# Strassen's scheme for the second product of a feed-forward stage

## The chip, the cores and the metric

One core of a Trainium2 chip. The metric is the device time of one execution in microseconds. A core has TensorE (matmuls, with a weight load before each), VectorE, ScalarE, GpSimd, and SyncE (SP), which here issues nearly all transfers. Memory on the chip is SBUF (128 partitions) and eight PSUM banks of 128 x 512 float32, into which TensorE accumulates.

## The reference

Five transformer layers in eight stages on 512 tokens of width 1024: `dil`, `diff`, `ev`, `x0`, `ff0`, `sw`, `x1`, `ff1`. The change touches the two feed-forward stages:

```
def squared_relu_mlp(u, w1, w2):
    return jnp.square(jax.nn.relu(u @ w1)) @ w2
...
        u = squared_relu_mlp(rms_norm(h, g_ff_pre[l]), w_ff1[l], w_ff2[l])
        h = h + rms_norm(u, g_ff_post[l])
```

Here `w1` is 1024 x 4096 and `w2` 4096 x 1024, so `y = relu(u w1)^2` is 512 x 4096. With float32 needed, each product is made of three: an operand is split into `hi` (rounded to the matmul's type) and `lo` (the rest), and hi hi, hi lo and lo hi are added (`mm3`).

## The kernel before

The weights come in one stream (`stream_order`, packed by the host as `ws[n]`, 128 x 2048): `cols` tiles are eight row blocks of 128 by 256 columns, `rows` tiles four row blocks by 512 columns. `weights(key)` (L262) hands out tile n, makes hi and lo of tile n+1 (`_split`, L249: ScalarE copies 1024 columns, VectorE subtracts, twice) and has tile n+2 loaded (`_dma`, L239: two transfers of 512 KB on SP through three `raw` buffers). `whi` and `wlo` are two buffers each of a whole tile.

A unit (`unit`, L307) is 128 features of the first product for all 512 tokens: 24 matmuls of 512 columns with the weights stationary. The first four units of a stage are begun (`begin`, L331) for tokens 0 to 255 at the end of the stage before it, while tokens 256 to 511 still go through the norm; `unit` then does the other half.

`ff` (L1211) works in four quarters q of 1024 features. In each, eight units are squared (ScalarE L1222, VectorE L1223) and split (`split_y`, L358); then the second product of this quarter is made for columns 0 to 511 and 512 to 1023 (c), in halves of the depth (kh), for four token tiles t, with four k each: 128 tokens of `y` stationary, 512 columns of weights moving. Each of its sums is added to `acc` in SBUF (VectorE L1247). In the last quarter, columns 512 to 1023 go through `second_half` (L462): a token tile at a time is finished, and `boundary` (L414) makes its norm and residual; the transposes of the next stage's input (`norm_T`, L382) are steps that are run between matmuls (L481, L485) and in `begin` (L350 and L347). `begin_out` (L434) loads the two gains.

Tile's framework makes all semaphores and the order on each engine; buffers of a tag are handed out as they fall free. GpSimd does part of the norms (L390, L376 to L379) and the rotations (L513) of other stages.

## Time and profile before

| what | value |
|---|---|
| median of 3 runs | 2400.42 us (2399.62 to 2403.36) |
| the profiled execution | 2402.01 us |
| its span, first to last instruction | 2400.2 us |
| granted TensorE clock, mean | 0.998 |
| busy: TensorE, VectorE, ScalarE, GpSimd | 2349.0, 1278.6, 930.4, 269.9 us |
| `ff0` lies at | about 1345 to 1702 us |
| `ff1` lies at | about 2053 to 2400 us |

A line of a group of instructions gives source line, engine, operation, out<-in, shapes and count, then busy time, the mean duration in ns, and the idle time before them with what ended it. A view of one line or tile gives durations as min/median/max in ns. A line of the timeline gives start and duration in us; a bracket at its end is the idle time before it and who ended it. Matmuls are pipelined: a listed duration of 0.39 us is not the time a matmul takes from the next; starts tell that.

### The profile page before, as it was taken

The page shows a single profiled execution, that of the slowest core. Times are in us where ns is not written, and L with a number is a line of the kernel's source. Part 1 is how long each engine was busy: PE and PEld are TensorE (multiplying, and loading weights), DVE is VectorE, ACT ScalarE, POOL GpSimd, SP SyncE. Part 2 cuts the span into 40 slices and gives each one's busy share as a digit, 9 for nine tenths or more (in the row PEclk, how much of TensorE's full clock was granted, in tenths as well). Part 3 has the DMA queues.
Part 4 walks back from the last instruction along what each step waited for, and adds up shares of the span by engine and source line. Part 5 has one row for each costly group of instructions (what it writes and reads, how often), then busy time and mean ns, then how long its engine had stood idle before and what let it go on. Part 6 is the DMA issues. An engine that isn't in the chain of part 4 may idle for free.

```text
span 2400.2 us, 33303 instructions
## 1 busy us (share of the span) xinstructions
PE 2349.0 (98%) x13008; PEld 1947.0 (81%) x13008; DVE 1278.6 (53%) x2370; ACT 930.4 (39%) x1843; POOL 269.9 (11%) x315
## 2 busy tenths in 40 slices
PE   7999999999999999999999999999999999999998
PEld 7879788787888878877988888888866988888887
DVE  5364655546665546664644633435786645533434
ACT  3333333333444444453533422323465534432322
POOL 3010111101211112000200100000211201000000
PEclk9999999999999999999999999999999999999999
DMA  5433333334232322223331332322322422332322
GB/s 167 129 102 119 98 116 91 108 93 129 99 100 86 98 91 93 76 70 114 123 123 71 106 101 92 104 90 88 99 84 97 141 89 80 106 105 89 103 90 79
DMA packets 94172, 242.39 MB, mean 101 GB/s; under 512 B 26700, under 2 KB 30828, under 8 KB 94016
## 3 DMA queue, kind: packets, MB, share of 16 engines
q1 hardware_dynamic: 93216, 238.34, 30.4%
q8 instruction: 102, 1.67, 0.3%
q0 software_dynamic: 800, 1.94, 0.3%
q14 instruction: 54, 0.44, 0.1%
HBM read 215.98 MB, written 4.33 MB: 92 GB/s over the span
## 4 chain that ended last, share of the span: by engine, by line
PE 63%; DVE 4%; issue 2%; ACT 2%; POOL 2%; DMA 1%; SPq 0%; POOLq 0%; DVEq 0%; ACTq 0%
PE pj L282 14%; PE pj L284 13%; PE pj L283 13%; PE sc L282 3%; PE sc L283 3%; PE sc L284 3%; PE pv L282 2%; PE pv L284 2%; PE pv L283 2%; PE sc L1325 1%; DVE h L431 1%; PE sc L775 1%; DVE wlo L258 1%; PE pv L797 1%; PE pt L401 1%
## 5 line engine op out<-in xcount | busy, mean ns | idle before, releaser
L258 DVE TENSOR_TENSOR wlo<-raw,whi 128x1024 fp32r<-128x1024 f32 x372 | 473.4, 1294 | 498.0 <-ACT whi L257 498.0
L257 ACT ACTIVATE whi<-raw 128x1024 fp32r<-128x1024 f32 x372 | 382.7, 1055 | 538.7 <-PE pj L284 216.7
L282 PE MATMUL pj<-uh,whi 128*128 128x512 f32 (+1 forms) x1424 | 561.4, 394 | 0.8 <-ACT ho L1101 0.8
L284 PE MATMUL pj<-uh,wlo 128*128 128x512 f32 (+1 forms) x1424 | 551.8, 388 | 1.6 <-DVE wlo L258 1.6
L283 PE MATMUL pj<-ul,whi 128*128 128x512 f32 (+1 forms) x1424 | 550.6, 387 | 0.0
L282 PEld LDWEIGHTS pj<-uh,whi 128*128 128x128 f32 x1424 | 267.6, 188 | 73.7 <-issue 17.1
L284 PEld LDWEIGHTS pj<-uh,wlo 128*128 128x128 f32 x1424 | 267.6, 188 | 60.0 <-issue 3.8
L283 PEld LDWEIGHTS pj<-ul,whi 128*128 128x128 f32 x1424 | 267.9, 188 | 52.1 <-issue 2.4
L513 POOL TENSOR_TENSOR ro<-rt 128x512 f32<-128x512 f32 x74 | 112.8, 1535 | 657.6 <-DVE rt L511 587.9
L282 PE MATMUL pj<-whi,uh 128*128 128x256 f32 x608 | 174.9, 288 | 0.0
L283 PE MATMUL pj<-wlo,uh 128*128 128x256 f32 x608 | 172.5, 284 | 0.0
L284 PE MATMUL pj<-whi,ul 128*128 128x256 f32 x608 | 171.9, 283 | 0.0
L282 PE MATMUL pj<-whi,yh 128*128 128x512 f32 x416 | 164.1, 395 | 1.4 <-ACT yh L355 1.1
L283 PE MATMUL pj<-wlo,yh 128*128 128x512 f32 x416 | 162.6, 391 | 0.9 <-DVE wlo L258 0.9
L284 PE MATMUL pj<-whi,yl 128*128 128x512 f32 x416 | 162.6, 391 | 0.0
L376 POOL TENSOR_SCALAR rs<-ss 128x1 f32<-128x1 f32 x32 | 23.1, 722 | 1089.0 <-ACT bq L422 1088.8
L282 PE MATMUL sc<-whi,yh 128*128 128x512 f32 x320 | 126.8, 396 | 0.1
L283 PE MATMUL sc<-wlo,yh 128*128 128x512 f32 x320 | 125.8, 393 | 0.0
L284 PE MATMUL sc<-whi,yl 128*128 128x512 f32 x320 | 125.2, 393 | 0.0
L282 PEld LDWEIGHTS pj<-whi,uh 128*128 128x128 f32 x608 | 116.4, 191 | 4.6 <-ACT at L231 2.3
L283 PEld LDWEIGHTS pj<-wlo,uh 128*128 128x128 f32 x608 | 116.5, 192 | 0.5 <-issue 0.2
L284 PEld LDWEIGHTS pj<-whi,ul 128*128 128x128 f32 x608 | 116.4, 192 | 0.2 <-issue 0.2
(364 smaller groups left out, 3833.4 us busy)
## 6 DMA issues: line engine op xcount, KB each, us to landing
raw<-in_ws_dram SPq DMA_DIRECT2D x372, 512.0 KB, 4.0
qk<-ro SPq DMA_DIRECT2D x256, 64.0 KB, 2.0
gpre<-in_gains_dram SPq DMA_DIRECT2D x8, 512.0 KB, 5.6
gpost<-in_gains_dram SPq DMA_DIRECT2D x8, 512.0 KB, 5.2
xt<-in_x_dram SPq DMA_DIRECT2D x4, 512.0 KB, 8.1
dv<-v SPq DMA_DIRECT2D x4, 512.0 KB, 4.1
v<-dv SPq DMA_DIRECT2D x16, 128.0 KB, 4.7
h<-in_x_dram SPq DMA_DIRECT2D x4, 512.0 KB, 5.6
```

The lines of the kernel that those rows point to most:

```text
L257: self.nc.scalar.activation(out=hi[:, s], in_=t, func=AF.Copy)
L258: self.nc.vector.tensor_sub(out=lo[:, s], in0=t, in1=hi[:, s].bitcast(F32))
L282: self.nc.tensor.matmul(ps, lhsT=ah, rhs=bh, start=first and k == 0, stop=False)
L283: self.nc.tensor.matmul(ps, lhsT=ah, rhs=bl, start=False, stop=False)
L284: self.nc.tensor.matmul(ps, lhsT=al, rhs=bh, start=False, stop=last and k == n - 1)
L376: nc.gpsimd.tensor_scalar(out=r[:, 0:1], in0=ss[:, 0:1], scalar1=ss[:, 1:2], scalar2=EPS, op0=ALU.add, op1=ALU.add)
L401: nc.tensor.transpose(pt[:, k * P:(k + 1) * P], b[:, (4 * g + k) * P:(4 * g + k + 1) * P], self.ident)
L431: nc.vector.scalar_tensor_tensor(out=h, in0=b, scalar=r, in1=h, op0=ALU.mult, op1=ALU.add)
L513: nc.gpsimd.tensor_tensor(out=o, in0=t[0], in1=t[1], op=op)
L775: nc.tensor.matmul(ps[:, :n], lhsT=q[hs, 0, i * P:n], rhs=q[hs, 1, :n], start=True, stop=True)
L797: nc.tensor.matmul(o[:, i * P:(i + 1) * P], lhsT=at[:, j * P:(j + 1) * P], rhs=v[h // 2][:, j, (h % 2) * P:(h % 2 + 1) * P], start=j == 0, ...
L1325: nc.tensor.matmul(ps[e][:, hp * 256 + lo:(hp + 1) * 256], lhsT=q[hs, hp, i * P:(i + 1) * P], rhs=kd[hs, g, (i - 1) * P + lo:(i + 1) * P], ...
```

## The change

The second product C = y W is cut into halves in tokens (256), in depth (each block of 512 features into two times 256) and in columns (512), and the eight half products become seven (Strassen's scheme in Winograd's form). With A11, A12 for tokens 0 to 255 and A21, A22 for tokens 256 to 511, S1 = A21 + A22, S2 = S1 - A11, S3 = A11 - A21, S4 = A12 - S2; T1 = B12 - B11, T2 = B22 - T1, T3 = B22 - B12, T4 = B21 - T2. The products are A11 B11, A12 B21, S1 T1 (first phase) and S4 B22, S2 T2, S3 T3, A22 T4 (second phase).

- The stage runs in eight blocks q of 512 features. `operands` squares with two ScalarE passes, keeps S2, S3, S4 and A22 of all features in SBUF, makes the four sums on GpSimd and splits A11, A12 and S1. `products(q - 1)` follows the four units of q and accumulates its three products over all depth in six PSUM banks.
- `block` loads the four quarters of a weight block, and GpSimd makes T3, T1, T2 and, once B21 is split, T4. `block_end` stores T2, T3, T4 to DRAM. The second phase reads them back through the weight stream, with B22 from `ws` again; its 32 steps accumulate on top of A11 B11's two banks (S2, S3, A22) or in two of their own (S4).
- The weight stream is handled in halves (`_load`, `_fill`, `_take`): four `whi` and `wlo` buffers of 1024 columns, with a loading depth of 2, or 3 inside `ff`.
- Tokens 0 to 255 get their `boundary` after S2, tokens 256 to 511 after A22, whose steps 3 and 5 hold the transposes of the first two token tiles. The scratch for descriptors of GpSimd's transfers is set to 4096.

```diff
@@ -84,10 +84,11 @@
         elif st in ("ff0", "ff1"):
-            for q in range(4):
-                for j in range(4):
-                    span("ff1_" + st[2], q * 1024 + j * 256)
-                outw("ff2_" + st[2], q * 1024)
+            for q in range(8):
+                for j in range(2):
+                    span("ff1_" + st[2], q * 512 + j * 256)
+                for m in range(2):
+                    out.append(("ff2_" + st[2], "quad", (q * 512 + m * P, m)))
...
         if kind == "cols":
             b = a[:, list(sel)].reshape(8, P, 256)
+        elif kind == "quad":
+
+            b = np.stack([a[sel[0] + 256 * j:sel[0] + 256 * j + P, 512 * c:512 * (c + 1)] for c in range(2) for j in range(2)])
...
+class Halved:
+
+
+    def __init__(self, parts):
+        self.parts = parts
+        self.n = parts[0].shape[1]
+
+    def __getitem__(self, key):
+        p, k, c = key
+        return self.parts[k // self.n][p, k % self.n, c]
+
+
@@ -195,6 +211,19 @@
         self.pos = 0
         self.wt = {}
+
+        self.halves, self.ready, self.loaded, self.done, self.depth = [], [], 0, 0, 2
+        blocks = []
+        for n, (_, kind, sel) in enumerate(self.order):
+            if kind != "quad":
+                self.halves += [(n, 0), (n, 1)]
+            elif sel[1] == 0:
+                blocks.append(n)
+                self.halves += [(b, name) for b in blocks[-2:-1] for name in ("B11", "T1", "B21")]
+                if len(blocks) == 8:
+                    late = [(b, name + "'") for name in ("B22", "T2", "T3", "T4") for b in blocks]
+                    self.halves += late[:5] + [(n, name) for name in ("B11", "T1", "B21")] + late[5:]
+                    blocks = []
...
 
-    def _dma(self, n):
...
-    def _split(self, n):
...
+    def _load(self):
+
+        while self.loaded < len(self.halves) and self.loaded < self.done + self.depth:
+            n, name = h = self.halves[self.loaded]
+            self.loaded += 1
+            if isinstance(name, str) and name[-1] != "'":
+                continue
+            r = self.wt[h] = self.wp.tile([P, 1024], F32, tag="raw", name="raw", bufs=3)
+            if name == "B22'":
+                src = self.a["ws"][n + 1, :, 1024:]
+            elif isinstance(name, str):
+                src = self.wt[n][name]
+            else:
+                src = self.a["ws"][n, :, name * 1024:(name + 1) * 1024]
+            self.nc.sync.dma_start(out=r, in_=src)
+
+    def _fill(self, m):
+
+        while len(self.ready) < m and self.done < len(self.halves):
+            self._load()
+            n, name = h = self.halves[self.done]
+            t = self.wt.pop(h) if h in self.wt else self.wt[n][name]
+            hi = self.wp.tile([P, 1024], F32R, tag="whi", name="whi", bufs=4)
+            lo = self.wp.tile([P, 1024], F32R, tag="wlo", name="wlo", bufs=4)
+            self.parts((hi, lo), t)
+            self.ready.append((hi, lo))
+            self.done += 1
+        self._load()
+
+    def _take(self, m, more=2):
+        self._fill(m + more)
+        got, self.ready = self.ready[:m], self.ready[m:]
+        return got
 
         self.pos += 1
-        self._split(n)
-        self._split(n + 1)
-        self._dma(n + 2)
-        hi, lo = self.wt.pop(n)
+        got = self._take(2)
         c = 256 if self.order[n][1] == "cols" else 512
-        return n, hi.rearrange("p (k c) -> p k c", c=c), lo.rearrange("p (k c) -> p k c", c=c)
-
-    def mm3(self, ps, pairs, first=True, last=True, between=None):
+        return n, *(Halved([g[x].rearrange("p (k c) -> p k c", c=c) for g in got]) for x in range(2))
+
+    def block(self, n, pool):
+
+        q = self.wt[n] = {}
+
+        def new(name):
+            q[name] = pool.tile([P, 1024], F32, tag="quad", name="quad", bufs=5)
+
+        for m, name in enumerate(("B11", "B12", "B21", "B22")):
+            new(name)
+            self.nc.sync.dma_start(out=q[name], in_=self.a["ws"][n + m // 2, :, (m % 2) * 1024:(m % 2 + 1) * 1024])
+        new("T3")
+        q["T1"], q["T2"], q["T4"] = q["B12"], q["B22"], q["B21"]
+        self.less(q["T3"], q["B22"], q["B12"])
+        self.less(q["T1"], q["B12"], q["B11"])
+        self.less(q["T2"], q["B22"], q["T1"])
+
+    def less(self, out, x, y):
+        self.nc.gpsimd.tensor_tensor(out=out, in0=x, in1=y, op=ALU.subtract)
+
+    def block_end(self, n):
+
+        q = self.wt[n]
+        self.less(q["T4"], q["B21"], q["T2"])
+        for name in ("T3", "T2", "T4"):
+            d = q[name + "'"] = self.dr.tile([P, 1024], F32, tag=name, name=name, bufs=8)
+            self.nc.sync.dma_start(out=d, in_=q[name])
+
+    def mm3(self, ps, pairs, first=True, last=True, between=None, **kw):
 
         n = len(pairs)
         for k, ((ah, al), (bh, bl)) in enumerate(pairs):
...
+            self.nc.tensor.matmul(ps, lhsT=ah, rhs=bh, start=first and k == 0, stop=False, **kw)
+            self.nc.tensor.matmul(ps, lhsT=ah, rhs=bl, start=False, stop=False, **kw)
+            self.nc.tensor.matmul(ps, lhsT=al, rhs=bh, start=False, stop=last and k == n - 1, **kw)
...
-    def begin(self, stage, last):
+    def begin(self, stage, last, tags=("sc", "sc", "pj", "pv")):
...
-            ps = self.ps(("sc", "sc", "pj", "pv")[n])
+            ps = self.ps(tags[n])
...
+        d = self.pair()
+        self.parts(d, y)
+        return d
+
+    def pair(self):
+        return [self.yp.tile([P, S], F32R, tag=t, name=t, bufs=8) for t in ("yh", "yl")]
 
...
-    def end_out(self):
+    def end_out(self, **kw):
         if self.next:
             self.u = self.u_next
-            self.begin(self.next, self.steps)
+            self.begin(self.next, self.steps, **kw)
...
 
     def ff(self, l, stage):
-        nc = self.nc
...
+        nc = self.nc
+        h = slice(0, 256), slice(256, S)
+        blocks = [self.order.index((f"ff2_{l}", "quad", (q * 512, 0))) for q in range(8)]
+        outer, inner, first = (ExitStack() for _ in range(3))
+        p = outer.enter_context(self.pool(f"ff{l}"))
+        self.depth = 3
+        left = {n: p.tile([P, 16, 256], F32, name=n) for n in ("S3", "A22")}
+        self.block(blocks[0], p)
+        p2 = inner.enter_context(self.pool(f"fs{l}"))
+        left.update({n: p2.tile([P, 16, 256], F32, name=n) for n in ("S4", "S2")})
+        p1 = first.enter_context(self.pool(f"fr{l}"))
+        banks = {}
+
+        def square(out, ps, tmp):
+            nc.scalar.activation(out=tmp, in_=ps, func=AF.Relu)
+            nc.scalar.activation(out=out, in_=tmp, func=AF.Square)
+
+        def operands(w, n, x2):
+
+            ps = self.unit(w, 0)
+            ya = p1.tile([P, S], F32, tag="ya", name="ya", bufs=2)
+            square(ya, ps, ya)
+            ps = self.unit(w, 1)
+            yb = p1.tile([P, 256], F32, tag="yb", name="yb", bufs=2)
+            square(yb, ps[:, h[0]], yb)
+            square(left["A22"][:, n], ps[:, h[1]], left["A22"][:, n])
+            s1 = p1.tile([P, 256], F32, tag="s1", name="s1", bufs=3)
+            for out, x, z, op in ((s1, ya[:, h[1]], left["A22"][:, n], ALU.add), (left["S2"][:, n], s1, ya[:, h[0]], ALU.subtract),
+                                  (left["S3"][:, n], ya[:, h[0]], ya[:, h[1]], ALU.subtract),
+                                  (left["S4"][:, n], yb, left["S2"][:, n], ALU.subtract)):
+                nc.gpsimd.tensor_tensor(out=out, in0=x, in1=z, op=op)
+            x1 = self.pair()
+            res = {"A11": [z[:, h[0]] for z in x1], "A12": [z[:, h[1]] for z in x1], "S1": [z[:, h[n % 2]] for z in x2]}
+            for name, src in (("A11", ya[:, h[0]]), ("A12", yb), ("S1", s1)):
+                self.parts(res[name], src)
+            return res
+
+        def products(q, ops):
+            for name in ("A11", "S1", "A12"):
+                (hi, lo), = self._take(1)
+                hi, lo = (z.rearrange("p (k c) -> p k c", c=512) for z in (hi, lo))
+                if q == 0:
+                    banks[name] = [self.ps(tag) for tag in {"A11": ("sc", "sc"), "A12": ("pt", "pt"), "S1": ("pv", "pj")}[name]]
+                for t in range(2):
+                    tok = slice(t * P, (t + 1) * P)
+                    self.mm3(banks[name][t], [([z[:, tok] for z in ops[j][name]], (hi[:, j, :], lo[:, j, :])) for j in range(2)],
+                             first=q == 0, skip_group_check=True)
+            self.block_end(blocks[q])
+            if q < 7:
+                self.block(blocks[q + 1], p)
+
+        ops = []
+        for q in range(8):
+            x2 = self.pair()
+            new = [operands(self.weights(f"ff1_{l}"), 2 * q + j, x2) for j in range(2)]
+            self.pos += 2
+            if q:
+                products(q - 1, ops)
+            ops = new
+        banks["S4"] = [self.ps("pj") for _ in range(2)]
+        acc, bo, late = {}, [], []
+        part = lambda t, c: acc[t][:, c * 512:(c + 1) * 512]
+        add = lambda out, ps: nc.vector.tensor_tensor(out=out, in0=out, in1=ps, op=ALU.add)
+
+        def done(name, t):
+            ps = banks[name if name == "S4" else "A11"][t]
+            if name in ("S4", "S2"):
+                add(part(t, 1), ps)
+            if name == "S2":
+                self.boundary(t, (part(t, 0), part(t, 1)), self.h[:, t, :], stage, bo[0])
+            elif name == "S3":
+                add(part(2 + t, 1), ps)
+            elif name == "A22":
+                self.boundary(2 + t, (ps, part(2 + t, 1)), self.h[:, 2 + t, :], stage, bo[0])
+
+        def go(name, i, t, y, w):
+            self.mm3(banks[name if name == "S4" else "A11"][t],
+                     [([z[:, j * 256 + t * P:j * 256 + (t + 1) * P] for z in y], [z[:, j, :] for z in w]) for j in range(2)],
+                     first=name == "S4" and i == 0, skip_group_check=True)
+            if i == 7:
+                done(name, t)
+
+        steps = [(name, i) for name in ("S4", "S2", "S3", "A22") for i in range(8)]
+
+        def split(k):
+            name, i = steps[k]
+            return self.split_y(left[name][:, 2 * i:2 * i + 2, :].rearrange("p k t -> p (k t)"))
+
+        ys = [split(0)]
+        for k, (name, i) in enumerate(steps):
+            if k == 5:
+                products(7, ops)
+                first.close()
+                acc.update({t: p.tile([P, D], F32, tag="quad", name="acc", bufs=5) for t in (2, 3, 0, 1)})
+                for t in range(2):
+                    self.copy(part(2 + t, 1), banks["S1"][t], "s")
+                for t in range(2):
+                    self.copy(part(t, 1), banks["S1"][t], "s")
+                    self.copy(part(t, 0), banks["A11"][t], "s")
+                    add(part(t, 0), banks["A12"][t])
+            lag = 2 if name == "A22" and i else 1
+            (hi, lo), = self._take(1, 3 - lag)
+            if k + 1 < len(steps):
+                ys.append(split(k + 1))
+            if (name, i) == ("S2", 7):
+                inner.close()
+                bo.append(outer.enter_context(self.pool("bo_" + stage)))
+                self.begin_out(stage, bo[0])
+            w = [z.rearrange("p (k c) -> p k c", c=512) for z in (hi, lo)]
+            y = ys.pop(0)
+            if name == "A22" and self.next and i in (3, 5):
+                self.steps.pop(0)()
+            go(name, i, 0, y, w)
+            while len(late) >= lag:
+                go(*late.pop(0))
+            late.append((name, i, 1, y, w))
+        for x in late:
+            go(*x)
+        self.depth = 2
+        self.end_out(tags=("pj", "pv", "sc", "sc"))
+        outer.close()
...
-                    self._dma(0)
+                    self._load()
...
-    nc = _bacc.Bacc("TRN2", target_bir_lowering=False, num_devices=1)
+    nc = _bacc.Bacc("TRN2", target_bir_lowering=False, num_devices=1, dynamic_dma_scratch_size=4096)
```

## Rows read from the trace of the kernel before

**Rows 1.** The page: span, busy time of each engine, granted clock in tenths.
```profile
span 2400.2 us, 33303 instructions
...
PE 2349.0 (98%) x13008; PEld 1947.0 (81%) x13008; DVE 1278.6 (53%) x2370; ACT 930.4 (39%) x1843; POOL 269.9 (11%) x315
...
PEclk9999999999999999999999999999999999999999
```

**Rows 2.** Windows of the first feed-forward stage: busy time by engine, clock, transfers.
```profile
core 0: us, PE busy (x) PEld busy (x) DVE busy (x) ACT busy (x) POOL busy (x), PEclk, DMA share, GB/s
...
1345.00:1702.00 357.00, 353.51 (x1661) 295.95 (x1659) 158.90 (x184) 117.45 (x164) 16.44 (x23) 1.00 0.28 95
...
1400.00:1500.00 100.00, 100.00 (x443) 82.81 (x442) 35.53 (x40) 29.65 (x38) 0.00 (x0) 1.00 0.28 95
...
1680.00:1690.00 10.00, 8.72 (x51) 7.15 (x51) 8.99 (x12) 6.82 (x13) 3.14 (x5) 1.00 0.28 99
1690.00:1700.00 10.00, 7.98 (x66) 7.60 (x65) 8.69 (x10) 5.45 (x11) 6.25 (x8) 1.00 0.24 79
```

**Rows 3.** Timeline of TensorE in that stage: first and last of 55 matmuls.
```profile
1399.91 0.39 PE L282 MATMUL pj<-whi,yh 128*128 128x512 f32 x1
...
1412.15 0.39 PE L282 MATMUL sc<-whi,yh 128*128 128x512 f32 x1
```

**Rows 4.** Groups of instructions by line and shape, whole span.
```profile
L513 POOL TENSOR_TENSOR ro<-rt 128x512 f32<-128x512 f32 x74 | 112.8, 1535 | 657.6 <-DVE rt L511 587.9 <-DVE ses L1332 20.7 <-DMA ot<-ds 20.7
...
L356 DVE TENSOR_TENSOR yl<-r,yh 128x512 fp32r<-128x512 f32 x64 | 43.9, 688 | 21.2 <-ACT yh L355 21.0
...
L390 POOL TENSOR_TENSOR bu<-h,gpre 128x320 f32<-128x320 f32 x28 | 37.1, 1327 | 53.1 <-DVE h L431 48.7 <-issue 4.4
...
L231 ACT ACTIVATE at<-pt 128x256 f32<-128x256 f32 x8 | 2.9, 365 | 0.0
```

**Rows 5.** Views of single lines: durations in ns, min/median/max.
```profile
L258 DVE TENSOR_TENSOR wlo<-raw,whi x372: 1197/1219/2337, 12.4 to 2373.5; 128x1024 fp32r<-128x1024 f32 x186
...
L513 POOL TENSOR_TENSOR ro<-rt x74: 1275/1305/2287, 38.2 to 1793.0; 128x512 f32<-128x512 f32 x74
...
L390 POOL TENSOR_TENSOR bu<-h,gpre x28: 876/1523/1584, 627.6 to 2049.0; 128x320 f32<-128x320 f32 x28
```

**Rows 6.** Timelines of GpSimd and VectorE in the first stage, where both work.
```profile
46.29 1.30 POOL L513 TENSOR_TENSOR ro<-rt 128x512 f32<-128x512 f32 x1 [2.63 <-DVE wlo L258]
47.90 1.92 POOL L513 TENSOR_TENSOR ro<-rt 128x512 f32<-128x512 f32 x1 [0.31 <-DMA qk<-ro]
...
46.73 1.93 DVE L258 TENSOR_TENSOR wlo<-raw,whi 128x1024 fp32r<-128x1024 f32 x1 [0.56 <-ACT whi L257]
```

**Rows 7.** Transfers: the queue, issues with time to landing, raw loads of 1400:1500.
```profile
q1 hardware_dynamic: 93216, 238.34, 30.4%
...
raw<-in_ws_dram SPq DMA_DIRECT2D x372, 512.0 KB, 4.0
...
gpre<-in_gains_dram SPq DMA_DIRECT2D x8, 512.0 KB, 5.6
...
dv<-v SPq DMA_DIRECT2D x4, 512.0 KB, 4.1
...
DMA to landing us min/median/max: 3.0/4.0/5.0
```

**Rows 8.** Timeline of ScalarE at the start of a second product.
```profile
2349.23 1.06 ACT L257 ACTIVATE whi<-raw 128x1024 fp32r<-128x1024 f32 x1 [3.17 <-PE pj L283]
2350.20 0.58 ACT L1222 ACTIVATE r<-pj 128x512 f32<-128x512 f32 x1
...
2352.18 0.63 ACT L355 ACTIVATE yh<-r 128x512 fp32r<-128x512 f32 x1 [0.46 <-DVE r L1223]
```

**Rows 9.** Timeline of TensorE at the end of the first feed-forward stage: the waits.
```profile
1683.76 1.16 PE L401 MATMUL pt<-ident,bu 128*128 128x128 f32 x8 [1.28 <-DVE ul L405]
...
1698.39 0.39 PE L284 MATMUL pj<-uh,wlo 128*128 128x256 f32 x1 [1.57 <-DVE wlo L258]
```

**Rows 10.** Timeline of VectorE after the last matmul.
```profile
2392.98 0.69 DVE L1231 TENSOR_TENSOR acc<-acc,pj 128x512 f32<-128x512 f32 x1 [1.50 <-PE pj L284]
```

More of the change, by code (lines that the diff above doesn't have):

```diff
@@ L236, in pool @@
             yield p
-    def _dma(self, n):
-        if n >= len(self.order) or ("r", n) in self.wt:
-            return
-        r = []
-        for half in range(2):
-            t = self.wp.tile([P, 1024], F32, tag="raw", name="raw", bufs=3)
-            self.nc.sync.dma_start(out=t, in_=self.a["ws"][n, :, half * 1024:(half + 1) * 1024])
-            r.append(t)
-        self.wt["r", n] = r
-    def _split(self, n):
-        if n >= len(self.order) or n in self.wt:
-            return
-        self._dma(n)
-        hi = self.wp.tile([P, 2048], F32R, tag="whi", name="whi", bufs=2)
-        lo = self.wp.tile([P, 2048], F32R, tag="wlo", name="wlo", bufs=2)
-        for half, t in enumerate(self.wt.pop(("r", n))):
-            s = slice(half * 1024, (half + 1) * 1024)
-            self.nc.scalar.activation(out=hi[:, s], in_=t, func=AF.Copy)
-            self.nc.vector.tensor_sub(out=lo[:, s], in0=t, in1=hi[:, s].bitcast(F32))
-        self.wt[n] = (hi, lo)
-        self.wt["r", n] = None
+    def _load(self):
[27 more added lines that the diff above has]
+        return got
     def weights(self, key):
@@ L358, in split_y @@
     def split_y(self, y):
-        hi = self.yp.tile([P, S], F32R, tag="yh", name="yh", bufs=8)
-        lo = self.yp.tile([P, S], F32R, tag="yl", name="yl", bufs=8)
-        self.parts((hi, lo), y)
-        return hi, lo
+        d = self.pair()
[3 more added lines that the diff above has]
+        return [self.yp.tile([P, S], F32R, tag=t, name=t, bufs=8) for t in ("yh", "yl")]
     def gain(self, pool, row, tag):
@@ L1212, in ff @@
         nc = self.nc
-        with self.pool(f"ff{l}") as p:
-            acc = [p.tile([P, D], F32, tag=f"acc{t}", name=f"acc{t}") for t in range(NT)]
-            for q in range(4):
-                y = []
-                for j in range(4):
-                    w = self.weights(f"ff1_{l}")
-                    for m in range(2):
-                        ps = self.unit(w, m)
-                        r = p.tile([P, S], F32, tag="r", name="r", bufs=2)
-                        nc.scalar.activation(out=r, in_=ps, func=AF.Relu)
-                        nc.vector.scalar_tensor_tensor(out=r, in0=ps, scalar=0.0, in1=r, op0=ALU.max, op1=ALU.mult)
-                        y.append(self.split_y(r))
-                if q == 3:
-                    self.begin_out(stage, p)
-                for c in range(2):
-                    cs = slice(c * 512, (c + 1) * 512)
-                    if q == 3 and c == 1:
-                        def done(t, ps):
-                            nc.vector.tensor_tensor(out=acc[t][:, cs], in0=acc[t][:, cs], in1=ps, op=ALU.add)
-                            self.boundary(t, (acc[t][:, :512], acc[t][:, 512:]), self.h[:, t, :], stage, p)
-                        self.second_half(f"ff2_{l}", y, done)
-                        continue
-                    pa = [self.ps(tag) for tag in ("sc", "sc", "pv", "pj")]
-                    for kh in range(2):
-                        _, hi, lo = self.weights(f"ff2_{l}")
-                        for t in range(NT):
-                            tok = slice(t * P, (t + 1) * P)
-                            self.mm3(pa[t], [((y[kh * 4 + k][0][:, tok], y[kh * 4 + k][1][:, tok]), (hi[:, k, :], lo[:, k, :]))
-                                             for k in range(4)], first=kh == 0, last=kh == 1)
-                    for t in range(NT):
-                        if q == 0:
-                            self.copy(acc[t][:, cs], pa[t])
-                        else:
-                            nc.vector.tensor_tensor(out=acc[t][:, cs], in0=acc[t][:, cs], in1=pa[t], op=ALU.add)
-            self.end_out()
```

3 lines of the change are left out of this document (removed).

## The prediction

> **What bounds the kernel now.** [...] A busy TensorE need not be at its peak, so I went to the windows of the first feed-forward stage: 353.5 us busy of 357, 100 of 100 in its middle, VectorE at 36%, ScalarE at 30%, GpSimd at nothing; the gaps lie at the stage's end (1.28 and 2.02 us in two slices of 10) [rows 2]. The timeline inside gives the price of a matmul with 512 columns: two starts with 54 matmuls between them lie 12.24 us apart, 0.2267 us each, and none waits [rows 3]. So a feed-forward stage is a count of matmuls times 0.2267. The sum below is made against the profiled execution's 2402.0 us (its span and 1.8 around it), 1.6 us above the median of the three runs.
>
> **What is removed.** A stage has 768 matmuls in its first product (32 units of 24) and 768 in its second (4 q, 2 c, 2 kh, 4 t, 4 k, 3 parts). The new second product is seven half-sized products of 8 blocks x 2 t x 2 j x 3 = 96, so 672, all with 512 columns and a 128x128 stationary tile as before. That is 96 fewer per stage, 192 in two stages: **-43.5 us** if TensorE stays fed. The removed accumulator additions are on VectorE, which is not the bound, and count nothing.
>
> **What the first phase costs other engines.** In an iteration q of 1 to 7, TensorE does four units (96) and three products (36): 132 matmuls, 29.92 us.
> - VectorE: seven weight halves at 1.22 (the median of L258) and six operand parts of 256 columns. No row has a 256-column subtract from SBUF; a line through 0.688 (512) and 1.22 (1024) gives 0.42 [rows 4, 5]. Sum 11.0 us.
> - ScalarE: seven copies at 1.06, and for each of two operand sets two 512-column passes at 0.63 [rows 8] and seven of 256 at 0.37 (a row of that size) [rows 4]. Sum 15.1 us, half of the time.
> - GpSimd: four subtractions of 1024 columns and eight of 256. The fastest runs of 512 and 320 columns took 1.275 and 0.876 [rows 5]; their line gives 2.34 and 0.74, sum 15.3 us. The upper bound is the mean under load, 1.535 and 1.327 [rows 4, 5], scaled to 3.07 and 1.06: 20.8 us.
> - These two do not run side by side. A 1.22 us subtract that started 0.44 us into a GpSimd addition took 1.93, and the next addition, started while that one ran, took 1.92 for 1.3 [rows 6]. Each waits for the other where both read two SBUF tensors, as all of these do. So VectorE and GpSimd share 26.3 us out of 29.92 (88%), 31.8 at the upper bound.
>
> I take the lower one, since the mean prices already hold the waiting that the sum counts again. What remains is lateness. A half is split (copy 1.06, subtract 1.22, about 2.5 with signals) once a `whi` buffer falls free, four halves deep; I count 5 to 8 us from that to its first matmul, so one subtraction of 2.34 in front of it is covered and two nearly. I take 0.2 us an iteration, **+3** for 14; bounds 0 and 26 (31.8 for 29.92).
>
> [...]
>
> **Queues.** Per iteration SP issues four raw loads, four block loads and three stores, 11 x 512 KB: 193 GB/s. Over the span that queue's 238 MB, 99 GB/s, take 30.4% of 16 engines [rows 7], so this takes 59%. A load lands in 4.0 us (3.0 to 5.0) in this stage, a store of this size in 4.1 [rows 7]. The stores of T3, T2 and T4 wait for GpSimd; behind them on SP stand the next block's loads and the raw loads, and behind T4 also those that reuse its buffer. From the split of B21 to that of the next T1: 1.22 + T4 2.34 + store 4.1 + load 4.0 + two subtractions 4.7 + copy and subtract 2.3 = 18.7 us of 29.92; there is room. ScalarE's copy of S1 waits for GpSimd, and weight copies stand behind it. But an engine's order is not that of the text: today a weight copy of L257, which the text asks for after the relu of L1222 and the copy of L355, runs before both [rows 8]; the framework places first what it expects to be ready. I count no stall here. Start of a stage: block 0's loads precede raw loads on SP, and nothing needs it for some 33 us (21.8 of four whole units, half of that for four begun ones): **+1**, bounds 0 and 5.
>
> **The second phase.** 32 steps of 12 matmuls, 2.72 us each. VectorE needs 1.22 + 0.69 = 1.91, ScalarE 1.06 + 0.63 = 1.69 [rows 4, 5, 8]; GpSimd is free. One raw load a step is again 193 GB/s through three buffers: landing 4.0, copy and subtract 2.3, signals and a wait behind a split of y about 1, so 7.3 us against 8.16; at a landing of 5.0 it is 8.3 and costs 0.05 a step. After S2 the gains come (512 KB each, 5.6 us [rows 7]), now in this dense stretch and with the boundary's VectorE work waiting for them; I take 1.5 us a stage, **+3**, bounds 0 and 10. At the turn, products(7) needs T1 of block 7 by about 24 us after products(6) began and the ring above gives some 19; six bank copies (ScalarE, 3.6 us) fall into three steps. **+2**, bounds 0 and 10. In A22 the lag of two leaves one half ready ahead: free to needed is 2.72 against 2.5, so a copy or subtract of y in front shows. **+2**, bounds 0 and 18 (0.63 + 0.69 in seven steps of two stages). S2, S3 and A22 follow each other in the same two banks, and VectorE has to add a bank (0.69) before the next product may write there. TensorE fills the time with one token tile of the other bank, 1.36 us; signals and a weight subtract of 1.22 that is under way make the addition late. Four such turns a stage: **+3**, bounds 0 and 10 (1.22 each).
>
> **The ends.** Tokens 0 to 255 are finished after S2, their transposes ride in A22. Today the first transposes wait 1.28 us and a weight's subtract 1.57 us among four boundaries crowded together [rows 9]; two boundaries remain. **-2.0**, bounds 0 and -3.5. At the last stage's end the accumulator addition (0.69) after the last matmul goes, since the bank is read directly [rows 10]: **-0.7**. Other stages only have their weight tiles freed in halves, hidden under TensorE's 98%: nothing, and the depth of loading is two halves as before.
>
> **Sum.** 2402.0 - 43.5 - 2.0 - 0.7 + 3 + 1 + 3 + 2 + 2 + 3 = 2369.8 for a profiled execution, less 1.6: **2368** for the median.
>
> **Rivals.**
> - *The shared port paces phase one.* At 31.8 us an iteration it adds 26 instead of 3: 2391. For it: the means under load. Against: these count waits twice.
> - *Slower: the ring closes in text order.* If ScalarE and GpSimd keep the order of the text, one ring holds everything: B21's subtract 1.22, T4 2.34, store 4.1, load 4.0, T3, T1, T2 7.0, s1 0.74, copy of S1 0.37, copies of B11 and T1 2.1, the operand's passes 1.2 + 1.5 + 0.7, s1 0.74, S1 0.37, copy of B21 1.06 = 27.5 us. With all other VectorE work (9.8 us) in GpSimd's way it is 37.2, 7.3 over TensorE's 29.92, times 14: +102 in place of my 3, 2467. It turns slower from about 32.8, that is with 5.3 of the 9.8. For it: one late signal moves the whole ring. Against: rows 8 show the order broken up, which cuts it at T1 to the 18.7 above.
> - *The gain is eaten.* Raw loads landing in 6 us under double traffic make a step 3.1 instead of 2.72: 62 steps x 0.38 = 24; with the turn at its bound (8 above mine) 2368 + 24 + 8 = 2400, no change. For it: the gains' loads take 5.6 [rows 7]. Against: the engines would be 59% busy, and 5.0 is the worst here.
>
> **Chances.** Forecast as argued (2355 to 2382) 0.70; the port paces (2382 to 2395) 0.13; lower than that by nearly all costs (below 2355) 0.04; eaten, 0.05; slower, 0.08. 0.2% (4.8 us) is about what a measurement of this kernel can tell. Faster 0.87, same 0.05, slower 0.08. The range is 2355 to 2394: the first case whole and most of the port's.
>
> **What would show it.** Right: 672 + 768 matmuls a stage at 0.2267, stages of about 315 us for 357, GpSimd busy 15 to 20 us of 29.92, TensorE's waits on `whi` and `wlo` of a few us in total. Wrong: GpSimd's 1024-column subtractions above 3 us, TensorE waiting for B21's or T1's split once an iteration, gaps of 2.72 us steps in phase two behind raw loads, or a granted clock that falls after such gaps, in which matmuls would take longer than 0.2267.

## The result and the profile after

The changed kernel takes **2358.88 us** (median of 4 runs, 2356.97 to 2361.64); beside it the kernel before took 2401.06. The ratio is 0.9824 [0.9807, 0.9841], that is 42 us less (38 to 46). The forecast was 2368, 33 us less by the same reckoning. The profiled execution took 2357.54 us where 2369.8 had been worked out.

The page of the changed kernel, the lines that answer to [rows 1]:
```profile
span 2355.5 us, 33967 instructions
...
PE 2309.4 (98%) x12816; PEld 1911.0 (81%) x12816; DVE 1386.0 (59%) x2410; ACT 1068.1 (45%) x2119; POOL 564.7 (24%) x507
...
PEclk9999999999999999999999999999999999999999
```
TensorE has 192 matmuls fewer and stays at 98%. The other three engines have 107, 138 and 295 us more to do.

Windows of the changed kernel: two of phase one of the first stage, the first 28 us of phase two behind its turn, and three around the turn of the second stage. The columns are those of [rows 2].
```profile
1400.00:1500.00 100.00, 100.00 (x443) 82.84 (x442) 48.18 (x44) 49.41 (x87) 59.00 (x41) 1.00 0.54 181
1500.00:1560.00 60.00, 60.00 (x266) 49.70 (x265) 30.18 (x29) 29.70 (x53) 35.59 (x25) 1.00 0.56 192
1574.00:1602.00 28.00, 28.00 (x125) 23.21 (x124) 23.76 (x27) 19.32 (x28) 2.40 (x1) 1.00 0.56 194
...
2254.00:2258.00 4.00, 1.89 (x9) 1.26 (x8) 4.00 (x3) 1.58 (x2) 1.99 (x1) 0.99 0.36 142
2258.00:2260.00 2.00, 2.00 (x6) 1.54 (x5) 2.00 (x3) 0.00 (x0) 0.00 (x0) 0.50 0.89 299
2260.00:2262.00 2.00, 2.00 (x7) 1.59 (x6) 0.71 (x2) 0.84 (x2) 0.00 (x0) 0.66 0.60 229
```
Phase one loses nothing: TensorE is busy 100 of 100 with GpSimd at 59, which is 17.7 us of an iteration of 29.92. In the second stage TensorE stood still for 2.1 us until 2257.12, and behind that the granted clock was 0.50 in one window of 2 us and 0.66 in the next, with matmuls starting 0.43 us apart for 0.23.

The views of single lines, durations in ns as in [rows 5], give the prices that had been taken from a line through other sizes:
```profile
L330 POOL TENSOR_TENSOR quad<-quad x64: 2393/2407/3488, 1348.2 to 2267.0; 128x1024 f32<-128x1024 f32 x64
...
L1310 POOL TENSOR_TENSOR S<-ya x32: 739/743/929, 1346.6 to 2235.8; 128x256 f32<-128x256 f32 x32
...
L1310 POOL TENSOR_TENSOR s<-ya,A x32: 737/1192/1719, 1354.8 to 2241.9; 128x256 f32<-128x256 f32 x32
```
A subtraction of 1024 columns takes 2.40 us undisturbed (taken: 2.34), one of 256 takes 0.74 (taken: 0.74).

The transfers of the changed kernel, as in [rows 7]:
```profile
q1 hardware_dynamic: 109344, 297.07, 38.4%
...
raw<-in_ws_dram SPq DMA_DIRECT2D x324, 512.0 KB, 3.7
quad<-in_ws_dram SPq DMA_DIRECT2D x64, 512.0 KB, 5.1
T<-quad SPq DMA_DIRECT2D x48, 512.0 KB, 3.0
raw<-T SPq DMA_DIRECT2D x48, 512.0 KB, 3.5
```
The sums come back from DRAM in 3.5 us, sooner than raw weights did before, and no matmul waits for a transfer in either stage.

What TensorE does wait for is at the turn to phase two. Timelines of TensorE, VectorE and GpSimd there, in the first stage:
```profile
1572.48 0.50 PE L347 MATMUL pj<-wlo,yh 128*128 128x512 f32 x1 [2.11 <-DVE wlo L420]
```
```profile
1562.28 1.21 DVE L420 TENSOR_TENSOR wlo<-raw,whi 128x1024 fp32r<-128x1024 f32 x1
1563.41 5.70 DVE L420 TENSOR_TENSOR yl<-S,yh 128x512 fp32r<-128x512 f32 x2
1569.04 3.39 DVE L420 TENSOR_TENSOR wlo<-raw,whi 128x1024 fp32r<-128x1024 f32 x1
```
```profile
1563.18 8.16 POOL L330 TENSOR_TENSOR quad<-quad 128x1024 f32<-128x1024 f32 x3 [2.51 <-DMA quad<-in_ws_dram]
```
GpSimd makes T3, T1 and T2 of the last block in one run of 8.16 us. VectorE gets one instruction in between two of them: two splits of 0.68 take 5.70, and the weight split of 1.22 takes 3.39. Steps of S4 come every 2.72 us and need 1.91 of VectorE, so there is no room to make up three such waits, and TensorE stands for 2.11. The second stage repeats it at 2257.12, again with 2.11. I call what the two engines take in turns the port; the traces show it in durations like these alone, and the last section says beside which instructions they grow.

The other new waits are the bank turns. TensorE in the first stage, where S2 gives way to S3 and S3 to A22, and VectorE at both of them:
```profile
1621.76 0.50 PE L346 MATMUL sc<-whi,yh 128*128 128x512 f32 x1 [0.45 <-DVE acc L1342]
...
1642.26 0.47 PE L346 MATMUL sc<-whi,yh 128*128 128x512 f32 x1 [1.59 <-DVE acc L1342]
```
```profile
1619.83 1.28 DVE L497 SCALAR_TENSOR_TENSOR h<-bz,rs,h 128x1024 f32<-128x1024 f32 x1 [0.85 <-POOL rs L445]
1621.03 0.68 DVE L1342 TENSOR_TENSOR acc<-acc,sc 128x512 f32<-128x512 f32 x1
...
1640.30 1.22 DVE L420 TENSOR_TENSOR wlo<-raw,whi 128x1024 fp32r<-128x1024 f32 x1
1641.44 0.68 DVE L1342 TENSOR_TENSOR acc<-acc,sc 128x512 f32<-128x512 f32 x1
```
At the second turn the addition of 0.68 starts behind a weight split that is under way, as the prediction had it. At the first one it starts behind the boundary's residual addition (L497, 1.28 us), and so it does at the one turn of the second stage that waits (L494, 1.42 us at 2306.09). That the boundary's work stands there too was not in the prediction.

### The profile page after: what moved, and what is told of

It reads as the page before. It is cut to its first block, busy times and chain, and to the rows that moved or that the text cites. A ratio compares the mean times of both kernels' runs of the same rounds, so it can differ in the third digit from the quotient of the medians.

```text
span 2355.5 us, 33967 instructions
## 1 busy us (share of the span) xinstructions
PE 2309.4 (98%) x12816; PEld 1911.0 (81%) x12816; DVE 1386.0 (59%) x2410; ACT 1068.1 (45%) x2119; POOL 564.7 (24%) x507
## 4 chain that ended last, share of the span: by engine, by line
PE 62%; DVE 5%; POOL 2%; issue 2%; ACT 1%; DMA 0%; DVEq 0%; POOLq 0%; SPq 0%; ACTq 0%
PE pj L346 13%; PE pj L347 13%; PE pj L348 13%; PE sc L346 3%; PE sc L347 3%; PE sc L348 3%; DVE wlo L420 1%; PE pv L346 1%; PE pv L348 1%; PE pv L347 1%; PE sc L1477 1%; PE sc L841 1%; DVE h L497 1%; PE pt L467 1%; POOL rs L445 1%
## 5 line engine op out<-in xcount | busy, mean ns | idle before, releaser
L420 DVE TENSOR_TENSOR wlo<-raw,whi 128x1024 fp32r<-128x1024 f32 x372 | 486.2, 1310 | 356.5 <-ACT whi L419 342.2
L419 ACT ACTIVATE whi<-raw 128x1024 fp32r<-128x1024 f32 x372 | 392.3, 1057 | 414.9 <-PE pj L347 129.9
L330 POOL TENSOR_TENSOR quad<-quad 128x1024 f32<-128x1024 f32 x64 | 172.7, 2698 | 94.6 <-DVE wlo L420 39.7
L346 PE MATMUL sc<-whi,yh 128*128 128x512 f32 x352 | 138.8, 394 | 2.7 <-DVE acc L1342 2.6
L347 PE MATMUL sc<-wlo,yh 128*128 128x512 f32 x352 | 138.3, 393 | 0.5 <-DVE wlo L420 0.5
L348 PE MATMUL sc<-whi,yl 128*128 128x512 f32 x352 | 137.8, 392 | 0.0
L347 PE MATMUL pj<-wlo,yh 128*128 128x512 f32 x336 | 132.2, 393 | 4.2 <-DVE wlo L420 4.2
L346 PE MATMUL pj<-whi,yh 128*128 128x512 f32 x336 | 133.1, 397 | 0.4 <-DVE bz L489 0.4
L348 PE MATMUL pj<-whi,yl 128*128 128x512 f32 x336 | 132.0, 393 | 0.0
```

The costliest lines, as they stand in the source:

```text
L330: self.nc.gpsimd.tensor_tensor(out=out, in0=x, in1=y, op=ALU.subtract)
L346: self.nc.tensor.matmul(ps, lhsT=ah, rhs=bh, start=first and k == 0, stop=False, **kw)
L347: self.nc.tensor.matmul(ps, lhsT=ah, rhs=bl, start=False, stop=False, **kw)
L348: self.nc.tensor.matmul(ps, lhsT=al, rhs=bh, start=False, stop=last and k == n - 1, **kw)
L419: self.nc.scalar.activation(out=dst[0], in_=src, func=AF.Copy)
L420: self.nc.vector.tensor_sub(out=dst[1], in0=src, in1=dst[0].bitcast(F32))
```

## The experiments

**The stream in halves alone.** The kernel before with the changed way of loading and splitting weights by halves, but the old feed-forward.
```diff
-    def _split(self, n):
+    def _fill(self, m):      (whi and wlo of 1024 columns, four buffers each, in place of 2048 and two)
...
 (ff, and the order of its weights, as before)
```


> The kernel before with one part of the change alone: the weight stream in halves (four whi and wlo buffers of 1024 columns), both products of the feed-forward stages as before. Between the two kernels the time outside the feed-forward stages also fell, by some 8 to 11 us of the landmarks, which the prediction put at nothing. Theory A: buffers freed by halves do that, since a weight split can start a quarter of a unit's matmuls earlier: 2390 to 2394 us, ratio about 0.996. Theory B: it comes from the new order of the schedule or the smaller descriptor scratch, not from the halves: 2399 to 2402, ratio 1.000.

Measured: 2394.71 beside 2401.52, ratio 0.9975 [0.9963, 0.9986]: 6 us less (3.4 to 8.9). The list of TensorE's waits:
```profile
PE pt L466 <- DVE bu L458: 18.2, 11, 11.2
...
PE pt L703 <- DVE PT L257: 0.8, 3, 0.3
```
Before, the same two groups stood at 22.4 and 3.1 us; a third went the other way, from 0.6 to 2.3 (VectorE's `pa` in front of the same transposes). The gain lies outside the feed-forward. Between matching matmuls of the two traces, the one with halves is 2.7 us ahead where the first feed-forward begins, 3.0 at its end, and 7.2 where the second begins.

The wait that shrinks most, 3.99 us before and 1.02 with halves, is at one transpose ahead of the first feed-forward. TensorE there, then VectorE, both in the kernel before, and VectorE with halves:
```profile
1128.88 1.17 PE L401 MATMUL pt<-ident,bu 128*128 128x128 f32 x8 [3.99 <-DVE bu L393]
```
```profile
1124.76 0.89 DVE L390 TENSOR_TENSOR bu<-mt,gmem 128x704 f32<-128x704 f32 x1 [8.25 <-DMA mt<-in_mem_dram]
```
```profile
1123.03 0.89 DVE L455 TENSOR_TENSOR bu<-mt,gmem 128x704 f32<-128x704 f32 x1 [4.86 <-DMA mt<-in_mem_dram]
```
VectorE waits there for a load (`mt`), not for a weight split, and with halves it starts 1.7 us earlier. The transpose starts 2.3 us earlier (1126.57), nearly the whole lead of 2.7. So the halves as a whole give the 6 us, but this piece comes for the most part through a transfer and not through a split that starts earlier.

**The scratch size alone.** The change also sets a DMA scratch size, which the run above left out; this is the kernel before with that one setting.
```diff
-num_devices=1)
+num_devices=1, dynamic_dma_scratch_size=4096)
```


> The kernel before, with nothing changed but the DMA scratch size that the change also sets (4096). Theory A, that the stream in halves as such saved the 6.5 us of the run with halves alone: this setting does nothing, 2400 to 2402, a ratio of 0.999 to 1.001. Theory B, that the smaller scratch is part of it (for instance through where other tiles come to lie): 2396 or less.

Measured: 2404.72 beside 2403.55, ratio 1.0002 [0.9993, 1.0011]. It shows no effect.

**The turn, mended in two ways.** First the weight sums on VectorE; then, with the sums left on GpSimd, another order: T1 first, and T2, T3, T4 after the block's products.
```diff
     def less(self, out, x, y):
-        self.nc.gpsimd.tensor_tensor(out=out, in0=x, in1=y, op=ALU.subtract)
+        self.nc.vector.tensor_tensor(out=out, in0=x, in1=y, op=ALU.subtract)
```
```diff
-        self.less(q["T3"], q["B22"], q["B12"])      (block)
         self.less(q["T1"], q["B12"], q["B11"])
-        self.less(q["T2"], q["B22"], q["T1"])
...
+        self.less(q["T2"], q["B22"], q["T1"])       (block_end)
+        self.less(q["T3"], q["T2"], q["B11"])
         self.less(q["T4"], q["B21"], q["T2"])
```


> The changed kernel with the four weight subtractions of a block (T3, T1, T2, T4) on VectorE instead of GpSimd. Theory A, the shared SBUF port makes the stall at the turn: VectorE then needs 11.0 + 4.9 = 15.9 us and GpSimd 5.9 of an iteration's 29.92, the burst of three 2.4 us subtractions is gone, and with it two waits of 2.1 us and the 1.9 us of lower clock after one of them: 2351 to 2355. Theory B, the turn waits for block 7's loads: the waits stay, 2357 to 2361. Theory C, VectorE's own queue becomes late when it does the sums: TensorE waits on wlo in every iteration, over 2365.

> The changed kernel with T1 alone computed when a block has landed; T2 = B22 - T1, T3 = T2 - B11 (the same matrix) and T4 follow together when the block's products have been issued. Theory A (port at the turn): VectorE meets one subtraction instead of three in the first steps of the second phase, the 2.1 us waits there go, 2353 to 2357. Rival: the burst only moves behind products(7), where six bank copies and the splits of S4 meet it, and a wait of 1 to 3 us comes back there: 2357 to 2362.

Measured: 2351.98, ratio 0.9795 [0.9782, 0.9808], with the sums on VectorE, and 2352.86, 0.9800 [0.9786, 0.9813], with T1 first. In both the two waits of 2.11 us are gone. The list of TensorE's waits with the sums on VectorE:
```profile
PE sc L346 <- DVE acc L1342: 2.7, 3, 1.6
...
PE sc L347 <- DVE wlo L420: 0.5, 2, 0.3
```
So the turn cost 6 to 7 us by the ratios' middles (the intervals still overlap a little). It is the burst of three on the port: the waits go when GpSimd has no part in it, and also when GpSimd does the same amount of work at another time with the block's loads as they were, so they were not waits for those loads.

**All sums on VectorE.** As above, with the operands' sums too.
```diff
-                nc.gpsimd.tensor_tensor(out=out, in0=x, in1=z, op=op)
+                nc.vector.tensor_tensor(out=out, in0=x, in1=z, op=op)
```


> All sums of the scheme, those of the operands too, on VectorE; GpSimd has no part in the feed-forward. VectorE then has seven splits of 1.22, six of 0.42, four subtractions of 1.22 and eight operations of 0.42 us in an iteration, 19.3 us of 29.92. Theory A, that what counts is the sum on the shared port and 19.3 is less than 26: the same as with the weights' sums alone on VectorE, 2351 to 2353. Theory B, that a queue of eight small operations in front of a weight split is what GpSimd kept away: waits on wlo once an iteration, 2356 to 2370.

Measured: 2354.65 beside 2403.55, ratio 0.9797 [0.9784, 0.9810], the same as with the weight sums alone. A window of phase one:
```profile
1400.00:1500.00 100.00, 100.00 (x443) 82.77 (x442) 59.28 (x85) 48.76 (x86) 0.00 (x0) 1.00 0.55 184
```
VectorE is busy 59.28 of 100 with everything. Alongside GpSimd it was 48.18 without the 12 sums of an iteration, which are 8.2 us undisturbed, 27 of 100: VectorE was spared 11 of them, and 16 came back as waiting. GpSimd is not needed for this change.

**The last step of S4 held back.** T1 first, and one step of S4 set between S2 and S3, so that matmuls on other banks cover that bank turn.
```diff
+        steps.insert(15, steps.pop(7))          (S4's step 7 after S2's; its weights likewise)
-            if name == "S2":
+            if name == "S4":                    (boundary of tokens 0 to 255)
```


> T1 first as in the run before (2352.9), and the last step of S4 is held back until after S2, so that 12 matmuls on other banks stand between the last of S2 and the first of S3; the boundaries of tokens 0 to 255 come 2.7 us later for it. Theory A, that the turn from S2 to S3 waits for VectorE's addition only for want of other work: its waits (0.45 and 0.58 us) go, 2351 to 2352.5. Theory B, that the later boundaries fall upon the turn from S3 to A22 or upon the transposes in A22 instead: the waits move there, 2353 to 2357.

Measured: 2353.39 beside 2403.55, ratio 0.9791 [0.9778, 0.9805]: not to be told from T1 first alone (0.9800). The list of TensorE's waits:
```profile
PE sc L347 <- DVE acc L1343: 1.6, 1, 1.6
PE sc L348 <- DVE wlo L421: 1.3, 1, 1.3
```
In the second stage the wait is gone. In the first it came back as 1.3 us for a weight split, close to what it replaced (0.45 for the addition and 0.5 for two splits). There VectorE has the boundaries' work, and moving the wait doesn't make it shorter: theory A for one stage; in the other the wait moved, but to an early step of S3 (1625.93) and not to the turn or the transposes that theory B names.

**How much the port bears.** T3 made three times, and five times, instead of once; then every weight half of phase one split twice.
```diff
+        for _ in range(3):                      (5 in the other kernel)
-        self.less(q["T3"], q["B22"], q["B12"])
+            self.less(q["T3"], q["B22"], q["B12"])
```
```diff
             self.parts((hi, lo), t)
+            if name in ("B11", "T1", "B21") or self.order[n][0][:4] == "ff1_":
+                self.nc.vector.tensor_sub(out=lo, in0=t, in1=hi.bitcast(F32))
```


> The subtraction for T3 is made three times instead of once, so GpSimd has two more of 2.4 us in each iteration. Theory A, that GpSimd and VectorE take the port in turns and nothing is lost until their sum passes TensorE's 29.92 us: by the sum of the prediction 26.3 + 4.8 = 31.1, and 0.4 less by what the run with four more showed, so 0.8 to 1.2 us for 14 iterations, plus a longer burst at the two turns, 2370 to 2378. Theory B, that lateness grows well before the port is full, half as much as with four more: 2395 to 2405. Theory C, that VectorE's splits only wait where they meet a subtraction and the mean of two is hidden: 2359 to 2362.

> The changed kernel with T3 computed five times in every block (the same values): four more GpSimd subtractions of 1024 columns, 9.6 us an iteration. Theory A, VectorE and GpSimd take turns on the port: their sum rises from 26.3 to 35.9 us against TensorE's 29.92, so about 6 us in each of 14 iterations, 2359 + 84 = 2443, and longer stalls at the turns. Theory B, only what happens to overlap is lost: GpSimd alone is busy 25 us of 29.92 and the time stays within 10 us of 2359.

> In phase one VectorE makes the low part of every weight half twice, seven more subtractions of 1.22 us an iteration; phase two and GpSimd's work are as they were. Theory A, that the sum on the port decides: 26.3 + 8.5 = 34.8 us in an iteration of 29.92, 14 times 4.9, 2415 to 2430. Theory B, that a ring through GpSimd decides, which is about 23.6 us long (T4 2.4, store and load 6.3, three subtractions 8, the rest 6.9): two of its steps are 1.2 longer and up to four of GpSimd's operations meet one VectorE instruction more, 27 to 31 us, 2359 to 2370.

Measured: 2374.31 (ratio 0.9876 [0.9863, 0.9890], 12 us over the changed kernel); 2445.14, one run; 2398.11 (ratio 0.9981 [0.9971, 0.9990], 38 us over). With two subtractions more, TensorE is busy 99.21 of 1400:1500, a loss of 0.24 us an iteration, and 5.6 us of waits, from start to start, stand at the first stage's turn in place of 2.3. So the 12 us fall in theory A's range, but most of them come from the turns and not from the iterations. With splits twice, where both theories missed (2415 to 2430 and 2359 to 2370), the same window:
```profile
1400.00:1500.00 100.00, 97.27 (x421) 78.19 (x421) 97.84 (x65) 45.03 (x81) 71.99 (x39) 1.00 0.53 184
```
VectorE has no time left (97.84 with its waiting), and the iterations, from one T4 to the next (1447.40 to 1478.84), are 31.44 us: 1.5 more in each of 14, which is 21 of the 38 us. To see the port itself I laid the intervals of all VectorE and GpSimd instructions over each other: the share of time in which at least one of the two runs. It is 81% in the changed kernel (72.6 of 1400:1490), 94% with two subtractions more, 95% with four more, and 99.7% with splits twice. So the port does pace TensorE when it is full, but its sum is not the plain sum of both engines' durations: 34.8 us were put in and took 31.4, and the changed kernel's 26.3 took 24.1 (81% of 29.92). A part of that lies in the durations themselves, since a listed duration overlaps the next: the split of 1.21 us at 1562.28 above is followed by VectorE's next instruction after 1.13. At 0.08 for each of VectorE's 20 instructions that is, as an estimate, 1.6 of the 3.4 us; the rest is not explained.

With four subtractions more, the 35.45 us from T4 to T4 fitted the port's sum of 35.9. The timelines of GpSimd and ScalarE there speak against that reading:
```profile
1455.15 3.31 POOL L331 TENSOR_TENSOR quad<-quad 128x1024 f32<-128x1024 f32 x1 [1.92 <-DVE wlo L421]
...
1464.77 18.95 POOL L331 TENSOR_TENSOR quad<-quad 128x1024 f32<-128x1024 f32 x7 [3.73 <-DMA quad<-in_ws_dram]
...
1490.60 2.41 POOL L331 TENSOR_TENSOR quad<-quad 128x1024 f32<-128x1024 f32 x1 [1.91 <-DVE wlo L421]
```
```profile
1481.32 1.06 ACT L420 ACTIVATE whi<-quad 128x1024 fp32r<-128x1024 f32 x1 [10.88 <-POOL quad L331]
```
GpSimd itself waits for a transfer and for VectorE, and ScalarE stands 10.88 us at the copy of T1 with the reading of the next unit's bank behind it: TensorE's waits there are for ScalarE to read a unit's bank, 36.4 us in 12. That looks like a chain of engines waiting for each other in order and not like a full port, though one of the port's two engines runs in 95% of the time; and the granted clock was 0.83 in 1480:1500 for 1.00 in the 40 us before (66 matmuls in 17.03 us of TensorE's busy time there, 82 in 18.57 in 1440:1460), so slower matmuls can be a part of the 35.45 too. The next kernel was to take the transfer out of the chain.

**The block loads ahead.** T3 five times as above, and the next block's loads written ahead of the products, into buffers of their own. To make room the kernel leaves S2 out: S4 lies in its buffers, and the product that uses S2 has S4 in its place.
```diff
         def products(q, ops):
+            if q < 7:
+                self.block(blocks[q + 1], p, None if q % 2 else p2)   (loads alone, two sets of buffers)
...
             self.block_end(blocks[q])
             if q < 7:
-                self.block(blocks[q + 1], p)
+                self.block_sums(blocks[q + 1])
```


> The subtraction for T3 is made five times, as in the run that gave 2445; but the next block's four loads go into buffers of their own and are issued ahead of the products, so that they no longer wait for T4 and its store. To make room S4 is kept in the buffers of S2, so the second product that uses S2 has S4 in its place; the number and size of all instructions stay. Theory A, that the shared port was full there (its sum was 35.9 us, the iteration 35.5): the port's work is the same, 2435 to 2450. Theory B, that the 35.5 us were a ring (T4 3.3, store and load 6.3, seven subtractions 19, the splits of T1 and B21 and what they wait for 6.9) and the port had time left: the ring is 6.3 shorter, iterations of 29.9 to 31, and with the long burst at the turn, 10 us or so a stage, 2365 to 2395.

Measured: 2484.81, one run; both theories missed, and on the same side. GpSimd, SP (stores of that block, loads of the next) and ScalarE:
```profile
1447.44 16.54 POOL L336 TENSOR_TENSOR quad<-quad 128x1024 f32<-128x1024 f32 x6 [7.68 <-DMA quad<-in_ws_dram]
```
```profile
1461.54 5.81 SPq L344 DMA_DIRECT2D T<-quad  x2
1467.45 1.21 SPq L322 DMA_DIRECT2D quad<-in_ws_dram  x2
1475.32 0.33 SPq L344 DMA_DIRECT2D T<-quad  x1
1475.69 0.42 SPq L322 DMA_DIRECT2D quad<-in_ws_dram  x1
1476.21 3.08 SPq L282 DMA_DIRECT2D raw<-in_ws_dram  x2
1479.39 0.38 SPq L322 DMA_DIRECT2D quad<-in_ws_dram  x1
```
```profile
1467.72 0.42 ACT L425 ACTIVATE yh<-s 128x256 fp32r<-128x256 f32 x1 [15.67 <-POOL s L1318]
```
The edit did not take the transfer out. On SP two of the four loads stand behind the stores of T3 and T2 (1461.54), the third behind T4's store (1475.32) and the fourth behind two raw loads as well. GpSimd's burst still waits 7.68 us for a load, and the next one 7.36. So this run does not test what the kernel would take without the transfer in the chain. The iteration is 37.8 us (1447.44 to the next burst at 1485.21). One of the port's engines runs in 88% of the time, so a full port is ruled out here. The copy of S1 on ScalarE waits 15.67 us for a 256-column sum that GpSimd has queued behind seven subtractions, six of them in the run above, and the weight copies stand behind it, B21's among them. TensorE's waits for those copies come to 68.2 us in 14. It is the closed ring of the prediction's slower rival, brought about by a longer burst: T4, its store, the load behind it, the burst, the small sum, the copies of S1 and B21, B21's split, T4. What the same load would take with loads that do run ahead, or with GpSimd's small sums put in front of the burst, was not tried, so for four subtractions more the shares of ring, port and clock stay open.

## Why the prediction was right, and where it was off

- **The matmuls, -43.5.** 12816 for 13008, and TensorE 100 of 100 in phase one at the same spacing. Right.
- **The port in phase one, +3; its rival, +26.** Measured 0. The prices were right (2.40 and 0.74 for 2.34 and 0.74), but adding both engines' durations overstates what the port needs by some 2 us in 26 and 3 in 35. Why the lateness costs nothing in an iteration (by the prediction, since halves are split ahead) is argued and not shown by a run of its own. With 31.1 us by the same sum an iteration lost 0.24 us, not 1.2.
- **The queue and the ring, 0.** No stall, as argued. 181 to 195 GB/s were moved for 193 worked out, and the engines' share was 0.54 to 0.58 for 59%. The block loads landed in 5.1 us for 4.0, the stores in 3.0 for 4.1. GpSimd's sums do hold ScalarE's copy of S1 up (39.7 us in 32 copies), without a wait on TensorE. The runs with T3 five times show that it becomes one when the burst is longer.
- **The turn, +2.** This term was undersized and had the wrong cause. It counted T1's way round the ring and the bank copies; what came late was a weight split behind three subtractions on the shared port. It cost 2.3 us from start to start in each stage, and in the second some 1.5 more at the lower clock (the spacing over 0.2267 in that stage sums to 5.3 us; 2.3 and 0.7 are the two waits, and with T1 first the remainder is 0.8). Together 6; removing it gave 6 to 7.
- **Gains in phase two +3, A22's lag +2, stage start +1.** None of them shows among TensorE's waits.
- **Bank turns, +3.** The three waits are 0.45, 1.59 and 0.58, which is 3.1 us from start to start, and 0.85 more for two splits behind the boundaries. Three turns wait of eight; one of them by the mechanism given, a weight split under way, and two behind the boundary's residual addition. The size came out right with a part of the cause missing.
- **The ends, -2.0 and -0.7.** At the first stage's end 0.6 us of excess spacing remain of 4.1 (the waits of [rows 9] among them), so -3.5, the bound. The tail after the last matmul went from 7.65 to 7.3 us: half the 0.7, since VectorE's first reading of the bank now waits 1.02 us for ScalarE's of the same bank.
- **"Other stages ... nothing."** This is the term that failed. The halves gave 6 us there (3.4 to 8.9). "Hidden under TensorE's 98%" was no argument: the other 2% are waits at the stages' seams, and those became shorter. The wait that shrank most, by 3.0 us, did so for the most part through a load that landed sooner. For the rest, that a weight split can start half a buffer earlier is likely and not shown.
- **"Stages of about 315 us for 357"** was false reckoning: 357 less 21.8 is 335. Measured 337: the last transposes at the first stage's end come 23.35 us earlier than before (1678.13 for 1701.48), of which 3.7 had been gained ahead of the stage.

The sum by what was measured: -43.5 for the matmuls, +6 for the turn, +4 for banks and splits, -3.5 and -0.35 for the ends, -6 for the halves, together -43.4. The profiled executions differ by 44.5, the medians by 42. The forecast's error (9 us by the medians, 12 by the profiled executions) is thus the halves (6), costs put 4 too high and ends put 1 too small. The range and the sign stood on the matmul count and on the order of the queues, and both held. There is luck in the sum of the costs: four terms put at 9 us together measured nothing, while the turn cost 4 more than its term. With the turn mended the same change takes 2352 to 2353 us, under the lower end of the range (2355).

## What to carry to other kernels

Where two engines hold each other up, as VectorE and GpSimd do here (a split of 1.22 us took 3.39), ask not only for the sum over an iteration but for the longest run of instructions on the one, and who on the other must deliver in that time: here the mean load of 81% cost nothing, and three subtractions in a row cost 6 us. Of several sums, make the one that is needed next first and the others in the slack behind the products (with T1 first the ratio was 0.9800 for 0.9824). TensorE at 98% did not hide the work at the seams here (the halves gave 6 us), so a change of granularity in a stream that runs through all stages is to be costed at each seam.

## What the runs showed of the hardware

- VectorE and GpSimd take turns by whole instructions, one for one, when both have a queue: the split of 1.22 us took 3.39 beside subtractions of 2.40, two of 0.68 took 5.70, and neither engine was shut out for the length of the other's run.
- It matters what VectorE reads. In the kernel before, its 148 products of the rotations (L511), each of a PSUM bank and an SBUF tensor, took 0.675 to 0.693 us, though 58 of them had a GpSimd addition (L513) beside them for more than half of that. Of those additions, the 14 with only such readers of PSUM beside them took 1.28 to 1.32 us, and of the 20 with only weight splits (L258, two SBUF tensors) beside them 19 took 2.13 to 2.29.
- The two engines' times do not simply add on the port: with at least one of them running 99.7% of the time, 34.8 us of work by undisturbed durations passed in 31.4 (about half of the difference is that listed durations overlap, by the estimate above).
- After the same wait of 2.11 us the granted clock fell to 0.50 and 0.66 in two windows of 2 us in the second stage, but not in the first stage of that execution (1.00 in 1572:1574 and 1574:1576).
